# Rotary embedding, interleaved pairs: one-row-block DMAs in strict store/load turns, and cos/sin tables read through a stride-0 operand

## Chip, cores, metric

One core of a Trainium2 chip. The metric is device microseconds of one execution, as the median of several runs. A run's span in its profile is about 2 us shorter than its measured time.

## The reference

`x` is float32 of shape (8, 2048, 16, 64) (batch, sequence, heads, head size), `cos` and `sin` are (2048, 32).

```python
x1, x2 = x_pairs[..., 0], x_pairs[..., 1]      # neighbouring elements of the last axis
out1 = x1 * cos - x2 * sin
out2 = x1 * sin + x2 * cos
out = np.stack([out1, out2], axis=-1).reshape(batch, seq_len, num_heads, head_dim)
```

The input and the output are 67.1 MB each in HBM. Each element is read once, takes part in three simple operations, and is written once.

## The kernel before

Each of 32 tiles is 2 MB of HBM: 128 partitions, four neighbouring sequence positions in each, so 16 KB of contiguous HBM per partition (called a row below). The load casts float32 to bfloat16 and the store casts back; both are issued from GpSimd's queue (the engine is POOL in the profiles, and the queue q0). The tables are copied out for all 16 heads by ScalarE.

```python
K = 4; G = S // (P * K); W = K * HD             # P = 128, HD = 1024
x_t = x.rearrange("b (g p k) h d -> (b g) p (k h d)", p=P, k=K)
...
for g in range(G):
    nc.sync.dma_start(out=cos_sb[:, g], in_=cos_g[g])     # pieces of 512 bytes
    nc.sync.dma_start(out=sin_sb[:, g], in_=sin_g[g])
...                                             # build_tables: c_tab, s_tab [P, W], every head
for g in range(G):
    c_tab, s_tab = build_tables(g)
    for b in range(B):
        nc.gpsimd.dma_start(out=xt, in_=x_t[i])           # 2 MB of HBM
        nc.vector.tensor_tensor(out=qt, in0=xt, in1=s_tab, op=mult)
        nc.vector.tensor_tensor(out=pt, in0=xt, in1=c_tab, op=mult)
        ...                                     # q_swap: qt with the two of a pair exchanged
        nc.vector.tensor_tensor(out=pt3, in0=pt3, in1=q_swap, op=add)
        nc.gpsimd.dma_start(out=out_t[i], in_=pt)
```

The framework's scheduler orders the instructions. From 57 us on it issues five stores, five loads, five stores, and so on.

## Time and profile before

| | before |
|---|---|
| time | 322.9 us |
| DMAs of x and out | 64 of 2 MB of HBM each, rows of 16 KB |
| HBM traffic over the span | 420 GB/s |
| DVE busy | 66% |
| first DVE operation | 10.4 us |

These are the lines of the profile's page for the kernel before: first the span, then the rows that cut the span into 40 slices (busy tenths; GB/s), then the DMA queues with packets, MB and share of 16 engines, and a line of the table of costly instructions (busy us, mean ns, idle before and its releaser). DVE is VectorE, ACT ScalarE, SP SyncE.

```profile
span 321.0 us, 304 instructions
...
DVE  0799887601999900999910999910899920899930
...
DMA  7999999999999999999999999999999999999994
GB/s 139 214 220 213 348 329 433 429 427 246 217 216 396 427 435 257 216 214 380 436 433 269 213 213 373 433 435 278 213 218 358 435 425 296 220 213 348 425 435 186
...
q0 software_dynamic: 9216, 100.67, 101.7%
q1 hardware_dynamic: 1152, 0.52, 0.8%
...
HBM read 67.63 MB, written 67.11 MB: 420 GB/s over the span
...
L78 DVE TENSOR_TENSOR qt<-xt,s_tab 128x4096 bf16<-128x4096 bf16 x32 | 73.0, 2285 | 79.7 <-DMA xt<-in_x_dram 79.7
```

The DMA row is full from the second slice to the last but one, while DVE has holes. DMA is therefore the bound. The GB/s row looks as if loads ran at half speed (213 against 433). That is because it counts bytes at the destination: a load reads 2 MB and writes 1 MB of bfloat16 (the records give a load row 8 KB and a store row 16 KB). In HBM bytes both directions run at about 430 GB/s. The trace's packet records (start, duration, size of each packet) say the same: in both phases an engine starts a 16 KB row about every 607 ns (the records carry no engine number; a pitch is 16 times the mean distance of the starts of all 16 engines).

### The profile page before, as it was taken

The page shows a single profiled execution, that of the slowest core. Times are in us where ns is not written, and L with a number is a line of the kernel's source. Part 1 is how long each engine was busy: PE and PEld are TensorE (multiplying, and loading weights), DVE is VectorE, ACT ScalarE, POOL GpSimd, SP SyncE. Part 2 cuts the span into 40 slices and gives each one's busy share as a digit, 9 for nine tenths or more (in the row PEclk, how much of TensorE's full clock was granted, in tenths as well). Part 3 has the DMA queues.
Part 4 walks back from the last instruction along what each step waited for, and adds up shares of the span by engine and source line. Part 5 has one row for each costly group of instructions (what it writes and reads, how often), then busy time and mean ns, then how long its engine had stood idle before and what let it go on. Part 6 is the DMA issues. An engine that isn't in the chain of part 4 may idle for free.

```text
span 321.0 us, 304 instructions
## 1 busy us (share of the span) xinstructions
DVE 213.1 (66%) x96; ACT 36.8 (11%) x49; POOL 34.4 (11%) x68
## 2 busy tenths in 40 slices
DVE  0799887601999900999910999910899920899930
ACT  8798100000820000000000000000000000000000
POOL 3010100400010030010030001030001030001000
DMA  7999999999999999999999999999999999999994
GB/s 139 214 220 213 348 329 433 429 427 246 217 216 396 427 435 257 216 214 380 436 433 269 213 213 373 433 435 278 213 218 358 435 425 296 220 213 348 425 435 186
DMA packets 10370, 101.21 MB, mean 315 GB/s; under 512 B 1152, under 2 KB 2176, under 8 KB 2176
## 3 DMA queue, kind: packets, MB, share of 16 engines
q0 software_dynamic: 9216, 100.67, 101.7%
q1 hardware_dynamic: 1152, 0.52, 0.8%
q14 instruction: 2, 0.02, 0.0%
HBM read 67.63 MB, written 67.11 MB: 420 GB/s over the span
## 4 chain that ended last, share of the span: by engine, by line
DVE 43%; DMA 32%; issue 15%; POOL 3%; ACT 2%; POOLq 0%; DVEq 0%
DMA xt<-in_x_dram 24%; DVE pt L84 17%; DVE qt L78 14%; DVE pt L79 13%; DMA out_dram<-pt 7%; POOL out_dram L86 1%; POOL xt L73 1%; ACT c_tab L61 1%; ACT s_tab L62 1%; DMA cos_sb<-in_cos_dram 1%; ACT s_tab L63 1%; POOLq L113 0%; POOLq L86 0%; DVEq L78 0%
## 5 line engine op out<-in xcount | busy, mean ns | idle before, releaser
L78 DVE TENSOR_TENSOR qt<-xt,s_tab 128x4096 bf16<-128x4096 bf16 x32 | 73.0, 2285 | 79.7 <-DMA xt<-in_x_dram 79.7
L79 DVE TENSOR_TENSOR pt<-xt,c_tab 128x4096 bf16<-128x4096 bf16 x32 | 73.1, 2283 | 14.5 <-ACT c_tab L61 10.4
L84 DVE TENSOR_TENSOR pt<-pt,qt 128x4096 bf16<-128x4096 bf16 x32 | 73.1, 2284 | 0.2
L86 POOL DMA_DIRECT2D out_dram<-pt x32 | 17.1, 534 | 260.1 <-DVE pt L84 260.1
L73 POOL DMA_DIRECT2D xt<-in_x_dram x32 | 17.2, 560 | 13.6 <-DVE qt L78 11.1
L62 ACT CAST s_tab<-sin_sb 128x512 bf16<-128x512 f32 x16 | 12.2, 764 | 52.0 <-DVE qt L78 48.2
L61 ACT CAST c_tab<-cos_sb 128x1024 bf16<-128x1024 f32 x16 | 16.2, 1025 | 0.7 <-DMA cos_sb<-in_cos_dram 0.7
L63 ACT ACTIVATE s_tab<-sin_sb 128x512 bf16<-128x512 f32 x16 | 12.2, 763 | 0.0
L61 ACT ACT_TABLE_LOAD x1 | 1.3, 1283 | 0.7 <-PEq L102 0.7
L102 POOL MEMSET const-float32-0.0<- 128x1 f32 x1 | 0.1, 99 | 0.2 <-issue 0.2
L102 POOL MEMSET const-bfloat16-1.0<- 128x1 bf16 x1 | 0.1, 102 | 0.0
L102 POOL MEMSET const-uint8-127<- 128x1 uint8 x1 | 0.1, 99 | 0.0
L102 POOL MEMSET const-float32-1.0<- 128x1 f32 x1 | 0.1, 98 | 0.0
## 6 DMA issues: line engine op xcount, KB each, us to landing
out_dram<-pt POOLq DMA_DIRECT2D x32, 2048.0 KB, 12.6
xt<-in_x_dram POOLq DMA_DIRECT2D x32, 1024.0 KB, 22.7
cos_sb<-in_cos_dram SPq DMA_DIRECT2D x4, 64.0 KB, 12.8
sin_sb<-in_sin_dram SPq DMA_DIRECT2D x4, 64.0 KB, 17.5
```

The costliest lines, as they stand in the source:

```text
L61: nc.scalar.copy(out=c_dst[:, k], in_=c_src)
L62: nc.scalar.copy(out=s_dst[:, k, :, :, 0], in_=s_src)
L63: nc.scalar.mul(out=s_dst[:, k, :, :, 1], in_=s_src, mul=-1.0)
L73: nc.gpsimd.dma_start(out=xt, in_=x_t[i])
L78: nc.vector.tensor_tensor(out=qt, in0=xt, in1=s_tab, op=mult)
L79: nc.vector.tensor_tensor(out=pt, in0=xt, in1=c_tab, op=mult)
L84: nc.vector.tensor_tensor(out=pt3, in0=pt3, in1=q_swap, op=add)
L86: nc.gpsimd.dma_start(out=out_t[i], in_=pt)
L102: nc = _bacc.Bacc("TRN2", target_bir_lowering=False, num_devices=1)
```

## The change

The intent is to keep loads and stores evenly mixed, to start computing sooner with smaller pieces, and to drop the table copies. A group is now four batches of one block of 128 sequence positions. Each block is its own DMA of 512 KB with rows of 4 KB. The tables stay at one copy for all heads, and the operand repeats them with a stride of 0. The order is fixed by hand.

```diff
-    x_t = x.rearrange("b (g p k) h d -> (b g) p (k h d)", p=P, k=K)
+    x_t = x.rearrange("b (t p) h d -> b t p (h d)", p=P)
...
-    for g in range(G):
-        nc.sync.dma_start(out=cos_sb[:, g], in_=cos_g[g])
-        nc.sync.dma_start(out=sin_sb[:, g], in_=sin_g[g])
-    def build_tables(g): ...
+    groups = [(t, b0) for t in range(T) for b0 in range(0, B, R)]     # R = 4
+    def load(g, r):  ...
+        nc.gpsimd.dma_start(out=tiles[g][:, r], in_=x_t[b0 + r, t])
+    def tab(a):
+        return a[:, t : t + 1].rearrange("p t i j -> p t (i j)").to_broadcast([P, R * H, D])
+    nc.vector.tensor_tensor(out=rows(qt), in0=rows(xt), in1=tab(s_tab), op=mult)
...
+    def store(g, r, pt):  ...
+        nc.gpsimd.dma_start(out=out_t[b0 + r, t], in_=pt[:, r])
+    with tc.manual_schedule():
+        nc.sync.dma_start(out=cos_sb, in_=cos_t)        # pieces of 128 bytes
+        nc.scalar.dma_start(out=sin_sb, in_=sin_t)
+        for g in range(LEAD):                           # LEAD = 4
+            for r in range(R):
+                load(g, r)
+        ...                                             # three ACT operations make the tables
+        for g in range(n):
+            pt = rotate(g)
+            for r in range(R):
+                store(g, r, pt)
+                if g + LEAD < n:
+                    load(g + LEAD, r)
```

More of the change, by code (lines that the diff above doesn't have):

```diff
@@ L26 @@
     P = 128
-    K = 4
-    G = S // (P * K)
     D2 = D // 2
     HD = H * D
-    W = K * HD
-    ntiles = B * G
-    TAIL_SPLIT = 0
-    x_t = x.rearrange("b (g p k) h d -> (b g) p (k h d)", p=P, k=K)
-    out_t = out.rearrange("b (g p k) h d -> (b g) p (k h d)", p=P, k=K)
-    cos_g = cos.rearrange("(g p k) c -> g p (k c)", p=P, k=K)
-    sin_g = sin.rearrange("(g p k) c -> g p (k c)", p=P, k=K)
-    consts = ctx.enter_context(tc.tile_pool(name="consts", bufs=1))
-    tabpool = ctx.enter_context(tc.tile_pool(name="tabpool", bufs=3))
@@ L43 @@
-    xpool = ctx.enter_context(tc.tile_pool(name="xpool", bufs=5))
-    qpool = ctx.enter_context(tc.tile_pool(name="qpool", bufs=4))
-    opool = ctx.enter_context(tc.tile_pool(name="opool", bufs=4))
-    cos_sb = consts.tile([P, G, K, D2], fp32)
-    sin_sb = consts.tile([P, G, K, D2], fp32)
-    for g in range(G):
-        nc.sync.dma_start(out=cos_sb[:, g], in_=cos_g[g])
-        nc.sync.dma_start(out=sin_sb[:, g], in_=sin_g[g])
-    def build_tables(g):
-        c_tab = tabpool.tile([P, W], bf16, name="c_tab")
-        s_tab = tabpool.tile([P, W], bf16, name="s_tab")
-        c_dst = c_tab.rearrange("p (k h i j) -> p k h i j", k=K, h=H, i=D2, j=2)
-        s_dst = s_tab.rearrange("p (k h i j) -> p k h i j", k=K, h=H, i=D2, j=2)
-        for k in range(K):
-            c_src = cos_sb[:, g, k : k + 1, :].to_broadcast([P, H, D2, 2])
-            s_src = sin_sb[:, g, k : k + 1, :].to_broadcast([P, H, D2])
-            nc.scalar.copy(out=c_dst[:, k], in_=c_src)
-            nc.scalar.copy(out=s_dst[:, k, :, :, 0], in_=s_src)
-            nc.scalar.mul(out=s_dst[:, k, :, :, 1], in_=s_src, mul=-1.0)
-        return c_tab, s_tab
@@ L66 @@
-    tile_idx = 0
-    for g in range(G):
-        c_tab, s_tab = build_tables(g)
-        for b in range(B):
-            i = b * G + g
-            xt = xpool.tile([P, W], bf16)
-            nc.gpsimd.dma_start(out=xt, in_=x_t[i])
-            qt = qpool.tile([P, W], bf16)
-            pt = opool.tile([P, W], bf16)
-            nc.vector.tensor_tensor(out=qt, in0=xt, in1=s_tab, op=mult)
-            nc.vector.tensor_tensor(out=pt, in0=xt, in1=c_tab, op=mult)
-            q_swap = dataclasses.replace(
-                qt, offset=qt.offset + 1, ap=[qt.ap[0], [2, W // 2], [-1, 2]]
-            )
-            pt3 = pt.rearrange("p (a j) -> p a j", a=W // 2, j=2)
-            nc.vector.tensor_tensor(out=pt3, in0=pt3, in1=q_swap, op=add)
-            nc.gpsimd.dma_start(out=out_t[i], in_=pt)
-            tile_idx += 1
+    T = S // P
@@ new lines @@
+    R = 4
+    LEAD = 4
+    x_t = x.rearrange("b (t p) h d -> b t p (h d)", p=P)
+    out_t = out.rearrange("b (t p) h d -> b t p (h d)", p=P)
+    cos_t = cos.rearrange("(t p) c -> p t c", p=P)
+    sin_t = sin.rearrange("(t p) c -> p t c", p=P)
+    consts = ctx.enter_context(tc.tile_pool(name="consts", bufs=1))
+    xpool = ctx.enter_context(tc.tile_pool(name="xpool", bufs=LEAD + 2))
+    qpool = ctx.enter_context(tc.tile_pool(name="qpool", bufs=2))
+    opool = ctx.enter_context(tc.tile_pool(name="opool", bufs=6))
@@ new lines, with load, rotate, rows @@
+    cos_sb = consts.tile([P, T, D2], fp32)
+    sin_sb = consts.tile([P, T, D2], fp32)
+    c_tab = consts.tile([P, T, D2, 2], bf16)
+    s_tab = consts.tile([P, T, D2, 2], bf16)
+    groups = [(t, b0) for t in range(T) for b0 in range(0, B, R)]
+    n = len(groups)
+    tiles = {}
+    def load(g, r):
+        t, b0 = groups[g]
+        if r == 0:
+            tiles[g] = xpool.tile([P, R, HD], bf16, name="xt")
+        nc.gpsimd.dma_start(out=tiles[g][:, r], in_=x_t[b0 + r, t])
+    def rotate(g):
+        t, _ = groups[g]
+        xt = tiles.pop(g)
+        qt = qpool.tile([P, R, HD], bf16, name="qt")
+        pt = opool.tile([P, R, HD], bf16, name="pt")
+        def rows(a):
+            return a.rearrange("p r (h e) -> p (r h) e", h=H, e=D)
+        def tab(a):
+            return a[:, t : t + 1].rearrange("p t i j -> p t (i j)").to_broadcast([P, R * H, D])
+        nc.vector.tensor_tensor(out=rows(qt), in0=rows(xt), in1=tab(s_tab), op=mult)
+        nc.vector.tensor_tensor(out=rows(pt), in0=rows(xt), in1=tab(c_tab), op=mult)
+        half = R * HD // 2
+        q_swap = dataclasses.replace(
+            qt, offset=qt.offset + 1, ap=[qt.ap[0], [2, half], [-1, 2]]
+        )
+        pt3 = pt.rearrange("p r (a j) -> p (r a) j", j=2)
+        nc.vector.tensor_tensor(out=pt3, in0=pt3, in1=q_swap, op=add)
+        return pt
@@ new lines, in store @@
+    def store(g, r, pt):
+        t, b0 = groups[g]
+        nc.gpsimd.dma_start(out=out_t[b0 + r, t], in_=pt[:, r])
[5 more added lines that the diff above has]
+                load(g, r)
+        nc.scalar.copy(
+            out=s_tab.rearrange("p t i j -> p (t i) j")[:, :, 0],
+            in_=sin_sb.rearrange("p t i -> p (t i)"),
+        )
+        nc.scalar.mul(
+            out=s_tab.rearrange("p t i j -> p (t i) j")[:, :, 1],
+            in_=sin_sb.rearrange("p t i -> p (t i)"),
+            mul=-1.0,
+        )
+        nc.scalar.copy(
+            out=c_tab.rearrange("p t i j -> p (t i) j"),
+            in_=cos_sb.rearrange("p t i -> p (t i)").to_broadcast([P, T * D2, 2]),
+        )
+        for g in range(n):
[4 more added lines that the diff above has]
+                    load(g + LEAD, r)
```

## The prediction

> **The bound now** is the DMA engines. The page's DMA row shows 9 tenths in 38 of 40 slices; the queue section gives the software queue 101.7% of 16 engines' span. The GB/s row swings between 213 and 433, but counts destination bytes: loads shrink float32 to bfloat16, stores grow it, so both move about 430 GB/s of HBM traffic (page: 420). DVE is 66% busy; 79.7 of its idle us wait for loads (waits view).
>
> In the DMA records an engine starts a 16 KB row every 607 ns, either way. Straight lines fitted to the packet starts on both sides of ten load/store turns jump by -15 to +38 ns per engine: nothing is gained when a store is followed by a load. So I expect no overlap of reads with writes.
>
> **Changes.**
> 1. DMAs: 64 (2 MB) become 256 (512 KB), same bytes. Each has a completion packet per engine (22 ns after loads, 42 ns after stores); from the start rate a DMA costs an engine 40 to 48 ns beyond its bytes (estimate). 192 more: +8 us.
> 2. Rows of 4 KB: 1,536 more packets per engine. [...]
> 3. Tables: cos and sin arrive as 4,096 pieces of 128 bytes, before 1,024 of 512. In the first 32 us now, small packets alternated one to one with load packets and stretched their pitch from 605 to 645 ns. At 25 to 30 ns for 128 bytes: +5 us of engine time.
> 4. The same turn-taking delays the tables: some 118 rounds of one load row (151 ns) and two small packets, 200 to 230 ns, put the sine table at 26 to 30 us (before, DVE started at 10.4). ACT then needs 1.5 us and three DVE operations 6.7, so the first store is issued near 36 to 39 us. The 16 loads ahead are done near 30 us, and the store blocks what follows in POOL's order: 5 to 8 us idle.
> 5. The instruction order rotates eight completion semaphores, so eight DMAs (10 us of work) are in flight; POOL's 256 issues of 0.54 us are 138 us. Neither binds.
> 6. DVE: the table operand repeats a row with stride 0. [...] 2.28 us per operation as now. ACT falls from 36.8 to about 4 us, worth nothing.
>
> **Critical path.** 1 to 4 lie on it (DMA is saturated); 5 and 6 do not. Sum: 323 + 8 + 4 + 5 + 6 = 346; 3 and 4 lean high, so I say 340 us, 328 to 350. Faster 0.06, same 0.10, slower 0.84.
>
> **Right if:** HBM traffic stays at 400 to 420 GB/s and load plus store packets per us are flat in steady state; first DVE operation near 28 us; a hole in the DMA row near 30 to 38 us; DVE operations 2.28 us; a row's pitch near 152 ns plus some 45 per DMA.
>
> **Wrong if:** short turns do let an engine read one row while writing another (then up to a quarter faster, with HBM traffic above 450 GB/s); 4 KB rows cost much more than 3 ns; the tables arrive early; or the repeated operand halves DVE's speed (370 us).

Two passages are cut from it, because no trace or run had shown what they rested on: in step 2 the cost of a row, and in step 6 the ground for an unchanged DVE time, which stays as the author's estimate. The sum came to 346 us (23 us above 323), shaded to 340. The +4 us in it are the term of step 2; without it the sum is 342 us. The figures for the changed kernel (the 25 to 30 ns of step 3, the rounds of step 4, the limits under "Wrong if") are estimates and not measurements.

## The result

The changed kernel takes **330.6 us** against 322.9 us. It is slower by 2.4%: the ratio is 1.0238, with a 95% interval of 1.0223 to 1.0252. Ratios here are the mean time of one kernel's fast runs over that of the other's in the same rounds, so they are not quite the ratio of the medians. The time lies inside the predicted range, but the predicted loss of 17 us was more than twice the real one of 7.7 us.

The same lines of the page, for the changed kernel:

```profile
span 328.6 us, 553 instructions
...
DVE  0699986686666786666876667866667866668710
...
DMA  9999999999999999999999999999999999999996
GB/s 159 209 215 324 312 307 320 321 307 313 323 312 307 321 319 308 313 323 312 307 321 319 308 315 323 310 307 322 318 308 315 323 310 308 323 316 309 411 421 201
...
q0 software_dynamic: 36864, 100.68, 115.2%
q10 hardware_dynamic: 2064, 0.26, 0.5%
q1 hardware_dynamic: 2064, 0.26, 0.5%
...
HBM read 67.63 MB, written 67.11 MB: 410 GB/s over the span
...
L72 DVE TENSOR_TENSOR qt<-xt,s_tab 128x4096 bf16<-128x4096 bf16 x32 | 73.3, 2291 | 95.1 <-DMA xt<-in_x_dram 95.1
```

There are three things to see.

- The GB/s row is flat near 315, so the mixing worked as intended. It is the average of the two old levels and not more, and HBM traffic fell from 420 to 410 GB/s.
- The DMA row has no hole near 30 to 38 us, where I had expected one.
- The share of 115.2% does not mean busier engines. Packet durations overlap at their ends: a 4 KB load row lasts 173 ns, but rows start about every 156 ns (before, 16 KB load rows lasted 625 ns at about 608). The share rises because there are more packets, and more overlaps, for the same bytes.

The timelines of the start show the tables (columns: start us, duration us, instruction, idle before and its releaser). First some lines of the kernel before, which goes on to issue eight table DMAs in all:

```profile
0.74 0.37 SPq L50 DMA_DIRECT2D cos_sb<-in_cos_dram  x1
1.17 0.42 SPq L51 DMA_DIRECT2D sin_sb<-in_sin_dram  x1
1.26 2.79 POOL L73 DMA_DIRECT2D xt<-in_x_dram  x5 [0.81 <-PEq L113]
...
10.39 2.29 DVE L79 TENSOR_TENSOR pt<-xt,c_tab 128x4096 bf16<-128x4096 bf16 x1 [10.39 <-ACT c_tab L61]
```

Then the changed kernel:

```profile
0.74 0.48 ACTq L88 DMA_DIRECT2D sin_sb<-in_sin_dram  x1
1.26 4.38 POOL L58 DMA_DIRECT2D xt<-in_x_dram  x8 [0.81 <-PEq L136]
...
7.54 0.76 ACT L92 CAST s_tab<-sin_sb 128x512 bf16<-128x512 f32 x1 [5.00 <-DMA sin_sb<-in_sin_dram]
...
11.37 2.29 DVE L72 TENSOR_TENSOR qt<-xt,s_tab 128x4096 bf16<-128x4096 bf16 x1 [11.37 <-DMA xt<-in_x_dram]
...
18.48 0.54 POOL L84 DMA_DIRECT2D out_dram<-pt  x1 [1.40 <-DVE pt L79]
```

The sine table was in at 7.5 us, where I had predicted 26 to 30. The first DVE operation did not wait for a table at all, but for its loads: an operation still covers a whole group of 2 MB, so the smaller DMAs did not start the computing sooner (11.4 us against 10.4). The first store was issued at 18.5 us, before the 16 loads were through.

Where the time went, from the packet records (all times from the start of the span; the rate is that of the middle, 80 to 280 us, with each row spread over the time it takes; "lost" is the time of a stretch less what its rows take at that rate):

```
                                        before      after
engine time per 2 MB of HBM, middle     4865 ns     4997 ns     x 64 = +8.4 us
first row starts at                     2.6 us      3.8 us
lost up to 80 us (first row included)   5.5 us      4.6 us      -0.8 us
lost from 280 us to the last row        0.5 us      1.2 us      +0.8 us
last row to the end of the span         3.8 us      2.9 us      -0.9 us
span                                    321.0 us    328.6 us    +7.5 us
```

Each span agrees with the sum of its terms to 0.1 us (differences are rounded after subtracting). The loss is all in the middle: the engines, full in both kernels, need 2.7% longer for the same bytes. The start is even a little better than before.

### The profile page after: what moved, and what is told of

It is laid out like the page before. It is cut to its first block, busy times and chain, and to the rows that moved or that the text cites. A ratio compares the mean times of both kernels' runs of the same rounds, so it can differ in the third digit from the quotient of the medians.

```text
span 328.6 us, 553 instructions
## 1 busy us (share of the span) xinstructions
DVE 216.7 (66%) x96; ACT 3.6 (1%) x4; POOL 136.9 (42%) x260
## 3 DMA queue, kind: packets, MB, share of 16 engines
q0 software_dynamic: 36864, 100.68, 115.2%
## 4 chain that ended last, share of the span: by engine, by line
DMA 88%; issue 5%; DVE 2%; POOL 2%; POOLq 0%; DVEq 0%; PEldq 0%
DMA xt<-in_x_dram 76%; DMA out_dram<-pt 12%; POOL xt L58 1%; DVE pt L79 1%; DVE qt L72 1%; DVE pt L73 1%; POOL out_dram L84 1%; POOLq L136 0%; DVEq L72 0%; PEldq L136 0%
## 5 line engine op out<-in xcount | busy, mean ns | idle before, releaser
L72 DVE TENSOR_TENSOR qt<-xt,s_tab 128x4096 bf16<-128x4096 bf16 x32 | 73.3, 2291 | 95.1 <-DMA xt<-in_x_dram 95.1
L84 POOL DMA_DIRECT2D out_dram<-pt x128 | 68.8, 537 | 104.1 <-DMA out_dram<-pt 97.0
L58 POOL DMA_DIRECT2D xt<-in_x_dram x128 | 68.0, 533 | 75.6 <-DMA xt<-in_x_dram 68.4
L73 DVE TENSOR_TENSOR pt<-xt,c_tab 128x4096 bf16<-128x4096 bf16 x32 | 73.1, 2284 | 0.0
L101 ACT CAST c_tab<-cos_sb 128x1024 bf16<-128x1024 f32 x1 | 1.0, 1017 | 0.0
L92 ACT CAST s_tab<-sin_sb 128x512 bf16<-128x512 f32 x1 | 0.8, 759 | 5.0 <-DMA sin_sb<-in_sin_dram 5.0
L96 ACT ACTIVATE s_tab<-sin_sb 128x512 bf16<-128x512 f32 x1 | 0.8, 758 | 0.0
```

The source lines that it names most:

```text
L58: nc.gpsimd.dma_start(out=tiles[g][:, r], in_=x_t[b0 + r, t])
L72: nc.vector.tensor_tensor(out=rows(qt), in0=rows(xt), in1=tab(s_tab), op=mult)
L73: nc.vector.tensor_tensor(out=rows(pt), in0=rows(xt), in1=tab(c_tab), op=mult)
L84: nc.gpsimd.dma_start(out=out_t[b0 + r, t], in_=pt[:, r])
L92: nc.scalar.copy(out=s_tab.rearrange("p t i j -> p (t i) j")[:, :, 0], in_=sin_sb.rearrange("p t i -> p (t i)"),)
L96: nc.scalar.mul(out=s_tab.rearrange("p t i j -> p (t i) j")[:, :, 1], in_=sin_sb.rearrange("p t i -> p (t i)"), mul=-1.0,)
```

## Experiments

Each kernel gave the right result. Edits are against the changed kernel.

### What makes the middle slower: 4 KB rows or 256 DMAs?

In the changed kernel both became four times as many. Three kernels fill the other cells of the table. Theory A is a cost per DMA, theory B a cost per row.

**4 KB rows, 2 MB per DMA:**

```diff
-        nc.gpsimd.dma_start(out=tiles[g][:, r], in_=x_t[b0 + r, t])
+            nc.gpsimd.dma_start(            # once per group, at r == 0
+                out=tiles[g], in_=x_t[b0 : b0 + R, t].rearrange("r p f -> p r f")
+            )
...                                          # the stores likewise
```

> The changed kernel, but the four row blocks of a group go in one DMA of 2 MB (64 DMAs in all, as before the change), still in 4 KB rows and strictly in turn. Theory A (a DMA costs each engine a fixed 40 to 48 ns beyond its bytes, whatever its rows): 192 DMAs less, 7 to 8 us less, 322 to 324 us. Theory B (each 4 KB row costs 2 to 4 ns more than its bytes): as the changed kernel, 329 to 331 us.

Measured: 325.2 us. This is neither A's number nor B's, but lies between them.

**16 KB rows, 512 KB per DMA** (32 partitions each):

```diff
-    x_t = x.rearrange("b (t p) h d -> b t p (h d)", p=P)
+    x_t = x.rearrange("b (g p k) h d -> b g p (k h d)", p=P, k=R)
...
-        nc.gpsimd.dma_start(out=tiles[g][:, r], in_=x_t[b0 + r, t])
+        ps = slice(r * Q, (r + 1) * Q)       # Q = 32
+        nc.gpsimd.dma_start(
+            out=tiles[g].rearrange("p r f -> p (r f)")[ps], in_=x_t[b, gg][ps]
+        )
...                                          # the stores likewise; tables in the same layout
```

> The changed kernel with 16 KB rows (four sequence rows per partition) but still 256 DMAs of 512 KB, each on 32 partitions, so two rows per engine and DMA, strictly in turn. Theory A (cost per DMA): 329 to 331 us. Theory B (cost per row): 322 to 324 us. If an engine's share of a 32-partition DMA is uneven, it is slower than both, and the rows per engine will show it.

Measured: 325.0 us, again between them. The rows per engine could not be counted, since the records carry no engine number; the rate below shows no loss from uneven shares.

**16 KB rows, 2 MB per DMA** (as the last one, but Q = 128, one DMA per group):

> The changed kernel with 16 KB rows and 64 DMAs of 2 MB, strictly in turn, tables by one DMA each and no copy per head: only the order of the DMAs and the tables differ from the kernel before. Theories A and B both: within 2 us of the kernel before, 321 to 324 us. If strict turns let reads and writes overlap at all, or cost something, this run differs from before by more than that.

Measured: 324.0 us, a ratio of 1.0029 to the kernel before, and within the expected 2 us.

Neither theory alone stands. The rates in the middle, which leave start and end aside, tell why (worked out from the packet records; rows and DMAs are per engine and 2 MB of HBM):

```
                       rows  DMAs   ns per 2 MB   HBM GB/s   time us
before                   8     1       4865         431       322.9
16 KB rows, 2 MB         8     1       4864         431       324.0
4 KB rows, 2 MB         32     1       4935         425       325.2
16 KB rows, 512 KB       8     4       4929         425       325.0
changed kernel          32     4       4997         420       330.6
```

The two costs add. A least-squares fit to these five rates gives 4820 ns + 2.9 ns per row + 21.1 ns per DMA, with no residual above 1 ns. (Three constants from four different pairs of rows and DMAs leave little to contradict the sum; two later runs test it.) From before to after this is 24 x 2.9 + 3 x 21.1 = 133 ns per 2 MB, or 4.4 us for the rows and 4.1 us for the DMAs over the 64 units of 2 MB.

The times agree less well with the rates: rows of 16 KB in 2 MB DMAs run at the rate of before and still take 1 us longer (1.4 us in the spans of the two profiles). The records put this at the end: 2.1 us are lost from 280 us to the last row instead of 0.5, as if the engines finished at different times (not shown, since the records carry no engine number). The start loses no more than before in all (5.3 and 5.5 us), though 0.6 us of it comes late, from 21 to 25 us, where about half of the load rows last 740 ns or more instead of 625. Why is open in both cases.

### Do the turns cost or gain anything?

```diff
-            pt = rotate(g)
-            for r in range(R):
-                store(g, r, pt)
-                if g + LEAD < n:
-                    load(g + LEAD, r)
+            pts.append((g, rotate(g)))
+            if len(pts) == LEAD:            # 16 stores, then 16 loads
+                for h, pt in pts:
+                    for r in range(R): store(h, r, pt)
+                for h, pt in pts:
+                    for r in range(R): ...  # load(h + LEAD, r)
+                pts = []
```

> The changed kernel with its DMAs in the order 16 stores, 16 loads instead of store, load, store, load. Theory A: turns cost and gain nothing, 329 to 332 us, steady packet rate as in the changed kernel (about 103 rows of 4 KB per us). Rival D (each turn from load to store costs the engines something): 8 us faster at most, near 323 us. Rival E (turns gain by overlap and hide a still larger cost per DMA): slower than the changed kernel by over 2 us with DMA still full.

Measured: 330.9 us, ratio 1.0238, the changed kernel's own ratio. These lines of its page show the order at work (slices; HBM traffic over the span):

```profile
DMA  9999999999999999999999999999999999999997
GB/s 163 209 216 422 421 294 209 243 419 422 269 210 267 422 420 244 210 292 420 424 217 209 318 419 406 209 211 341 424 378 210 209 369 419 355 209 209 394 422 237
...
HBM read 67.63 MB, written 67.11 MB: 411 GB/s over the span
```

The GB/s row swings between 209 and 422 again, and nothing else changes: 4997 ns per 2 MB in both. So strict turns give nothing and cost nothing. One might have hoped that a store's writes hide a load's reads. In none of these runs does a mix of loads and stores move more HBM bytes than either alone (in the row above 209 for loads is 418 GB/s of HBM, and stores have 422; over the span it is 411).

### Why was there no hole at the start?

The prediction had the tables' small pieces take turns with load rows for 25 us. In the changed kernel the packet records show a piece taking 13 ns, and 2,943 of the 4,096 pieces starting before the first load row at 3.8 us. With one issue per table (0.42 and 0.48 us), the cosine pieces started from 1.8 to 3.9 us and the sine pieces from 2.5 to 7.2 us. To test this, the same pieces are issued in 16 DMAs per table:

```diff
-        nc.sync.dma_start(out=cos_sb, in_=cos_t)
-        nc.scalar.dma_start(out=sin_sb, in_=sin_t)
+        for t in range(T):                  # T = 16
+            nc.sync.dma_start(out=cos_sb[:, t], in_=cos_t[:, t])
+            nc.scalar.dma_start(out=sin_sb[:, t], in_=sin_t[:, t])
```

> The changed kernel with its cos and sin tables in 16 DMAs each (one 128-byte piece per partition and DMA) instead of one DMA each; the pieces and bytes are the same. Theory H (in the changed kernel the tables came early because one issue queued all 2,048 pieces before the first load row, at 13 ns a piece; the turn-taking that the prediction counted on needs pieces that come after the loads): issues of 0.45 us put only some 5 to 7 of 16 DMAs per table ahead of the loads, the rest takes turns with load rows, the sine table lands at 15 to 25 us instead of 7, the first DVE operation starts 5 us or more later than 11.4, and the kernel takes 331 to 336 us. Rival (small pieces are served ahead of load rows whatever the issue): tables still before 9 us, time 330 to 331.

Measured: 344.2 us, 13.6 us slower than the changed kernel, even slower than expected. These are its slices, the first ones being the point, and lines of its timeline:

```profile
DVE  0006999987666577666667766666776666577610
...
DMA  7991799999999999999999999999999999999995
GB/s 122 200 198 31 169 314 319 310 320 310 321 309 315 317 311 319 310 320 310 318 315 312 319 310 320 310 319 314 314 316 312 319 310 319 311 317 315 400 422 183
```

```profile
0.73 19.84 ACTq L89 DMA_DIRECT2D sin_sb<-in_sin_dram  x16
...
17.15 0.53 POOL L58 DMA_DIRECT2D xt<-in_x_dram  x1 [1.00 <-DMA xt<-in_x_dram]
26.36 1.28 ACT L93 ACT_TABLE_LOAD   x1 [26.36 <-DMA sin_sb<-in_sin_dram]
...
29.08 2.29 DVE L72 TENSOR_TENSOR qt<-xt,s_tab 128x4096 bf16<-128x4096 bf16 x1 [29.08 <-ACT s_tab L97]
...
36.19 0.54 POOL L84 DMA_DIRECT2D out_dram<-pt  x1 [18.52 <-DVE pt L79]
```

This is what the prediction described, one change of the issue away. The last table piece lands at 25.6 us, DVE starts at 29.1, the first store is issued at 36.2. No row starts from 27.9 to 37.3 us, because the last of the 16 loads is issued at 17.2 us and POOL's next instruction is a store that waits 18.5 us for DVE. Between 6 and 24 us the records count 87 load rows, 83 cosine and 83 sine pieces per us, and the starts of load rows recur at 185, 365 and 550 ns, as if each engine served one of each in turn (the records carry no engine number). A load row then comes every 185 ns instead of 156, so a piece costs about 15 ns (half of the 29). The middle is as in the changed kernel (4997 ns per 2 MB). Theory H holds. Its time was missed by 8 us because I put the tables at 15 to 25 us and counted no stand-still after them. I had also expected 5 to 7 DMAs per table ahead of the loads; only two were (256 pieces each). Six per queue were issued by 3.7 us, and the later ones came only every 1.5 us, about the time in which 128 pieces pass at 83 per us, so the turns seem to set the pace of the issues too.

### Does the sum hold further out, and where does the in-flight limit bind?

```diff
-        nc.gpsimd.dma_start(out=tiles[g][:, r], in_=x_t[b0 + r, t])
+        for h in (slice(0, 64), slice(64, 128)):
+            nc.gpsimd.dma_start(out=tiles[g][h, r], in_=x_t[b0 + r, t][h])
...                                          # the stores likewise
```

> The changed kernel with each 512 KB DMA cut in two of 64 partitions: 512 DMAs of 256 KB, 4 KB rows as in it. From the four runs of rows and sizes I have a sum: each DMA costs an engine 20 to 23 ns and each row 2.6 to 3.0 ns beyond its bytes, the two add. This predicts 256 more DMAs, 5 to 6 us more than the changed kernel, 335 to 337 us, with HBM traffic near 413 GB/s in the middle. If instead eight DMAs in flight (now 5 us of work) or POOL's issues (some 250 us) bind, DMA engines will show gaps and the time is over 340 us.

Measured: 341.7 us, not the sum's 335 to 337. Yet the sum holds where DMA is full: between 105 and 160 us the rate is 5083 ns per 2 MB (413 GB/s of HBM traffic), and the fit, which did not use this run, gives 4820 + 32 x 2.9 + 8 x 21.1 = 5082. The rest comes from gaps, as the rival has it, but from stalls of POOL that it did not foresee. Two views show it, the chain of work that ended last, by its shares, and the timeline around one of the stalls (columns as above):

```profile
POOL 66%; issue 18%; DMA 10%; DVE 4%; POOLq 0%; DVEq 0%; PEldq 0%
```

```profile
79.62 1.18 POOL L86 DMA_DIRECT2D out_dram<-pt  x2 [0.18 <-issue]
80.77 2.29 DVE L80 TENSOR_TENSOR pt<-pt,qt 128x4096 bf16<-128x4096 bf16 x1
80.85 1.13 POOL L59 DMA_DIRECT2D xt<-in_x_dram  x2
85.36 1.07 POOL L86 DMA_DIRECT2D out_dram<-pt  x2 [3.38 <-issue]
86.42 1.05 POOL L59 DMA_DIRECT2D xt<-in_x_dram  x2
```

POOL stood still for 3.4 us with no wait that the profile shows, and the DMA engines then thinned out (287 GB/s of HBM traffic from 85 to 90 us, and 410 to 420 before). POOL, now 79% busy, took 4.2 us over the next eight issues (85.4 to 89.5 us). There are four such stalls (2.8 to 3.4 us). The changed kernel's POOL has two such stalls as well (3.2 us at most), and its DMA row shows nothing of them. There POOL issued eight loads from 1.3 us without a wait, and the ninth, at 7.3 us, waited for a landing, as did 235 of the 248 issues after the eighth. As an estimate from the rates, eight DMAs of 512 KB are 10 us of work in flight (8 x 4997 / 4 ns), eight of 256 KB only 5 (8 x 5083 / 8 ns). What causes the stalls is open, but they follow the number of issues and not the time: here they come after issues 128, 249, 370 and 491, and in the changed kernel after 113 and 219, as in the two other kernels with its DMAs, though up to 15 us apart in time. How much of the loss is POOL's issues and how much the limit of eight was not tested apart.

### A version that beats both

The sum says how to go the other way: fewer and longer rows, fewer DMAs. Rows of 32 KB in 4 MB DMAs (`k=8`, three loads ahead), tables by one DMA each and no copy per head:

> 16 KB rows made 32 KB, 32 DMAs of 4 MB, strictly in turn, tables by one DMA each and no copy per head, three loads ahead. The sum of costs per row and per DMA predicts 1.4 us less engine time than 16 KB rows in 2 MB DMAs: 321 to 323.5 us if the start and the end cost no more than there.

Measured: 321.5 us, ratio to before 0.9951 (0.9939 to 0.9964). The middle runs at 4841 ns per 2 MB; the fit, which did not use this run, says 4820 + 4 x 2.9 + 0.5 x 21.1 = 4842. With the sequence laid out so that a table row is 2 KB (edit against the run just told; the stores and the tables likewise):

```diff
-    x_t = x.rearrange("b (g p k) h d -> b g p (k h d)", p=P, k=R)
+    x_t = x.rearrange("b (p g k) h d -> b g p (k h d)", p=P, k=R)
```

> As the 32 KB rows in 4 MB DMAs, with the sequence laid out so that a partition holds 16 neighbouring positions: the tables then come as 128 rows of 2 KB each instead of 256 of 1 KB. Engine time for the tables falls by under 1 us: 320.5 to 323 us, at best 0.7 per cent below the kernel before. If rows 64 KB or more apart in HBM are slower to read, the rate in the middle falls below 431 GB/s.

Measured: 320.9 us, ratio 0.9934 (0.9917 to 0.9952). The rate in the middle is the same (4841 ns), so the greater distance between rows cost nothing here. Both beat the kernel before, but by less than 1%. That the second beats the first is not shown: their intervals overlap.

## Why the prediction was wrong

The direction, the bound and the mechanism of the steady part were right. The size was not: what steps 3 and 4 charged for the tables (11 us of the sum) did not come, and step 1 was twice too large (4 us too much). That the time still lay inside the range is due to the range's width and says nothing for these steps. Point by point, in the prediction's own numbering:

- **No overlap of reads with writes: right.** The order of 16 stores and 16 loads has the same rate as strict turns (4997 ns per 2 MB in both).
- **Step 1, "40 to 48 ns beyond its bytes", +8 us: twice too large.** A DMA costs an engine 21.1 ns, so 192 more cost 4.1 us. The 40 to 48 ns were my estimate of the excess over the bytes in the trace of before, which by itself does not show the time of the bytes. With the fit's 4820 ns, the excess is 4865 - 4820 = 45 ns, and it also holds the cost of the eight rows of the DMA (8 x 2.9 = 23 ns), which I then charged again in step 2.
- **Step 2, rows of 4 KB, +4 us: right in size.** It was 2.9 ns per row (the fit) and 4.4 us.
- **Step 3, "25 to 30 ns for 128 bytes", +5 us: wrong.** My estimate started from the 40 ns (605 to 645) by which a 512-byte piece had stretched a load row's pitch. A 128-byte piece took 13 ns, and most pieces ran before the first load row. The first row came at 3.8 us instead of 2.6 (probably behind the pieces; not tested alone), but the pieces no longer stretched 30 us of loads as the 512-byte pieces had in the kernel before. The whole start became 0.8 us cheaper.
- **Step 4, the late tables and the 5 to 8 us hole: the failing step.** The prediction had the sine table at 26 to 30 us and 5 to 8 us of idle DMA; the table was in at 7.5 us and no hole appeared. The turn-taking itself is real (87 load rows to 83 and 83 pieces per us with 16 DMAs per table), but I took "some 118 rounds" still to come behind the loads from a trace in which the tables were issued in eight small DMAs, 0.4 us or more apart. With one large DMA per table, 2,943 of the 4,096 pieces started before the first load row. With 16 DMAs per table the predicted sequence appears almost to the number (DVE at 29.1 us, first store at 36.2 us, 9.4 us without a new row).
- **Step 5, in-flight limit and POOL: right** for 256 DMAs (POOL 42% busy, and a full DMA row). With 512, POOL's stalls are no longer hidden (the chain that ended last is 66% POOL); which of the two binds was not tested apart.
- **Step 6, DVE: right.** The two multiplications take 2,291 and 2,284 ns with the stride-0 operand, and 2,285 and 2,283 without. ACT fell from 36.8 to 3.6 us, and the run with 16 KB rows and 2 MB DMAs, which has no copies either, is no faster than before (324.0 us).

In sum: 8 + 4 + 5 + 6 = 23 us predicted (shaded to 17), and 4.1 + 4.4 - 0.8 (start) - 0.1 (end) = 7.6 us from the measured terms, beside 7.7 us measured.

## What to carry to other kernels

When the DMA engines are full, count what each engine executes: here bytes at 27.2 GB/s (128 KB per engine in the fit's 4820 ns), plus 2.9 ns per row, plus 21 ns per DMA. (All runs cast, and the bytes are those of float32 in HBM; without a cast this was not measured.) The order of loads and stores did not enter (4997 ns per 2 MB in turns and in blocks of sixteen), and smaller DMAs took away no wait here (first DVE operation at 11.4 us, before 10.4), so they only cost. The delay of the tables beside the stream of loads depended on how they were issued: the last piece came at 7.2 us with one DMA per table and at 25.6 us with 16 (330.6 and 344.2 us in all). So issue tables whole and first; do not carry a waiting time over from a kernel that issued them differently.
